# Strassen matrix product on one core: when s4's quarter sums are made, and a fourth sum of s3 that goes through DRAM

## The chip, the cores and the metric

One core of a Trainium2 chip runs the kernel. The metric is the device time of one launch in microseconds; the runs shown are three, with their median. Engines are named as the profile names them: PE is TensorE (matmuls; its weight loads are PEld), DVE is VectorE, ACT is ScalarE, POOL is GpSimd, SP is SyncE, which here only issues DMAs.

## The reference

```python
m, k, n = 4096, 4096, 4096          # a, b: float32, alpha = 0.01
def reference(a, b, alpha):
    x = np.matmul(a, b)
    return np.where(x > 0, x, alpha * x)
```

## The kernel before

The product is computed in float16 with float32 sums. The output is cut into four groups of 1024 rows (g = 0 to 3) and four strips of 1024 columns (j = 0 to 3). One group and one strip together are a region; its product has the full inner size of 4096. A region is computed by the Winograd form of Strassen's method: A's part is cut into a11, a12, a21, a22 and B's part into B11, B12, B21, B22, and seven products of half the size take the place of eight. The sums of A are s1 = a21 + a22, s2 = s1 - a11, s3 = a11 - a21 and s4 = a12 - s2; those of B are made in place. The list PRODUCTS gives the order: a11, a12, s2, s3, s1, a22, s4. A whole product is 64 matmuls of 128x512 (some 13.8 us). Three of the seven can be split once more by the same method, "in quarters": seven small products of 16 matmuls of 128x256 (12.2 us). That is done for product 3 (s3) in `fourth_in_quarters`, product 5 (a22) in `sixth_in_quarters` and product 6 (s4) in `seventh_in_quarters`. Each needs four quarter sums of its A operand (sx[1] to sx[4]) and three of its B operand (t(2), t(4), t(1)). The products are numbered from 0, as in the code.

The loop over `regions` is unrolled. Within a group the order of strips is 2, 0, 3, 1 (in the last group 2, 0, 1, 3). The text names a region (g, j). The first regions of a group are (1,2), (2,2) and (3,2), the second ones (1,0), (2,0) and (3,0). In a first region product 3 is whole; in the second and third, and in the fourth of groups 1 and 2, it is in quarters.

Nothing is reordered by a scheduler: the pools are under a manual schedule, each engine runs its instructions in the order in which the code issues them, and a wait is put where a tile's earlier writers or readers demand it. So an instruction that waits holds up everything behind it on its engine or DMA queue. DMAs are issued from three queues: SP (stores of the output, what is kept in DRAM and brought back), ACT (the loads of s4's kept sums) and POOL (A and B from the inputs, converted to float16 on the way). All of them share 16 DMA engines.

What the change touches:

- `sums_of_a(g, name, room)` makes the four quarter sums of a22 or s4 on DVE (L700, 128x2048 each) and stores each on SP into `kept_q` in DRAM (L701). `room(n)` gives the tile for sum n. The later products load the sums from DRAM: a22's by `load_sums` on SP, s4's by `following` within `sixth_in_quarters` on ACT (both L743).
- `new_a16()` takes a tile of 512 KB from a pool of three that also serves the loads of A and the squares of the measures. `x_pool` holds three tiles of 2 MB: s1, s2 and s4; after product 2, s2's place becomes `t`, four quarter tiles t[:, 0] to t[:, 3], for quarter sums of B and one of A.
- `keep_x21` stores a quarter of s4 or a22 to DRAM in groups 1 and 2 (L716), since its place is used for s3's sums.
- `sums_of_s3` makes s3's quarter sums (L734): 1 and 3 at the end of a first region, 2 and 4 in the second. The fourth is stored on SP (`kept_s3`, L736); the third and fourth regions load it from there (L1071, L1108), the second region uses it from where it was made.
- `b_sum` (L588) makes the sums of B: behind product 0 the two of B12 and then those of B11 that become t2, the operand of product 2 (two halves, `ks`; product 2 takes them one after the other); behind product 1 B21; behind product 2 the operand of product 4. `t3_of_b` (L680) and `sums_of_b` (L686, L688, L690) make the quarter sums of B.
- `measure` objects square tiles of B on ACT (L230) and add them up on DVE (L239 to L263), for a check of the values' sizes. `early` are those around product 0 (one in (1,0), two in (2,0), none in (3,0)), `middle` the one behind it (in (3,0): B22).
- `leave(u1_pairs, 0, 0)` applies the leaky ReLU (L312) to what product 1 finished (L967 adds the banks) and stores it in four DMAs on SP (L978).
- `load_s2` (L770) brings s2 back from DRAM in two halves, the second behind the first sum of B. `fetch_b` issues the sixteen loads of the next region's B from POOL (L532), four for each of B12, B11, B21, B22 in this order, as soon as the products free their places.

Of the kernel before, what the change touches and what calls it, by code (L numbers as in the profile page):

```python
# [47 lines left out]
def kernel(  # L48
# [402 lines left out]
    for i in range(1, len(steps)):  # L451
        t, h, u, first, last = steps[i]
# [19 lines left out]
        t, h, u, first, last = steps[i]  # L472
# [117 lines left out]
    def measure(i, which, x, y):  # L590

        if which:
            tiles = [have_b[i, 2 * x + k, y] for k in ((1, 0) if regions[i][0] else (0, 1))]
        else:
            tiles = [at[regions[i][0], x, 2 * y + k] for k in range(2)]
        parts = halves(tiles[0]) + halves(tiles[1])
        if tiles[0] is first_a:
            return MeasureFirst(which, parts, None)
        return Measure(which, parts, not which)
# [71 lines left out]
    def quarters_of_b(i, half, nt):  # L671
        return {(k, n): have_b[i, 2 * half + k, nt][:, :, n * HALF:(n + 1) * HALF]
                for k in range(2) for n in range(2)}

    def quarters_of_a(g, name):
        return {(h, k): operand(g, name, k)[:, :, h * HALF:(h + 1) * HALF, :] for h in range(2) for k in range(2)}

    def t3_of_b(y):

        nc.vector.tensor_tensor(y[0, 1], y[1, 1], y[0, 1], SUB)  # L680

    def sums_of_b(y, to, some=(2, 4, 1)):
        tt = nc.vector.tensor_tensor
        f = lambda n: b_quarter(to[n])
        if 2 in some:
            tt(f(2), y[0, 1], y[0, 0], ADD)  # L686
        if 4 in some:
            tt(f(4), y[1, 0], f(2), SUB)  # L688
        if 1 in some:
            tt(f(1), y[1, 1], f(2), SUB)  # L690

    def sums_of_a(g, name, room):

        x = {key: q.rearrange("p c m e -> p c (m e)") for key, q in quarters_of_a(g, name).items()}
        made = {}

        def make(n, x0, x1, op):
            made[n] = room(n)
            f = lambda t: made[t].rearrange("p (c m) -> p c m", m=2 * HALF) if isinstance(t, int) else x[t]
            nc.vector.tensor_tensor(f(n), f(x0), f(x1), op)  # L700
            nc.sync.dma_start(kept_q[name][n - 1], made[n])  # L701

        make(1, (1, 0), (1, 1), ADD)
        make(2, 1, (0, 0), SUB)
        make(3, (0, 0), (1, 0), SUB)
        make(4, (0, 1), 2, SUB)

    def x21(g, name):
        return operand(g, name, 0)[:, :, HALF:, :]

    def by_chunk(t):
        return t.rearrange("p c m e -> p c (m e)") if len(t.shape) == 4 else t.rearrange("p (c m) -> p c m", m=2 * HALF)

    def keep_x21(g, name):
        if g < G - 1:
            nc.sync.dma_start(by_chunk(kept_x21[name]), by_chunk(x21(g, name)))  # L716
# [7 lines left out]
    def sums_of_s3(g, some, room=None):  # L724

        x = {key: by_chunk(q) for key, q in quarters_of_a(g, "s3").items()}
        rooms = s3_rooms(g)
        sx = {n: by_chunk(room) for n, room in rooms.items()}
        for n in some:
            if n == 4:  # L730
                sx[4] = by_chunk(room)
            x0, x1, op = {1: (x[1, 0], x[1, 1], ADD), 2: (sx[1], x[0, 0], SUB),
                          3: (x[0, 0], x[1, 0], SUB), 4: (x[0, 1], sx[2], SUB)}[n]
            nc.vector.tensor_tensor(sx[n], x0, x1, op)  # L734
            if n == 4:
                nc.sync.dma_start(kept_s3, room)  # L736

    def s3_rooms(g):
        return {1: x21(g, "a22"), 2: x21(g, "s4"), 3: x21(g, "s3")}
# [22 lines left out]
    def new_a16(_=None):  # L762
        return a16_pool.tile([P, QUARTER], DT, name="q16", tag="a16")
# [18 lines left out]
    for i, (g, j) in enumerate(regions):  # L782
# [210 lines left out]
        def fetch_a(h, half, n):  # L993
            if n == 0:
                coming["rows", h, half] = small_pool.tile([P, 16], FP32, name="rows", tag=f"rows{half}")
            coming[h, half][n][0]()
# [21 lines left out]
        first_of_group = i == 0 or regions[i - 1][0] != g  # L1018
        in_quarters = g > 0 and not turning
        in_fourth = in_quarters and not first_of_group  # L1020
        second_of_group = in_fourth and regions[i - 2][0] != g
        early = [measure(i, *block) for block in EARLY.get((g, j), [])]
# [8 lines left out]
        for n, m in enumerate(early):  # L1031
            if n:
                m.begin()
            m.end()
        have_t2 = g > 1 and j == CACHED
        if have_t2:
            for k in ks:
                t = have_b[i, k, 0] = b_pool.tile([P, KC, NT], DT, name="b", tag="b11")
# [28 lines left out]
        if in_fourth:  # L1067
            tq = {n: new_a16() for n in (2, 4)}
            sx4 = new_a16()
            if not second_of_group:  # L1070
                nc.sync.dma_start(sx4, kept_s3)  # L1071
            t3_of_b(quarters_of_b(i, 0, 1))
            sums_of_b(quarters_of_b(i, 0, 1), tq, (2,))
            if second_of_group:
                sums_of_s3(g, (4,), sx4)
            sums_of_b(quarters_of_b(i, 0, 1), tq, (4,))
        if (g, j) == (0, LAST):
# [7 lines left out]
        if turning and g:  # L1085
            t3_of_b(quarters_of_b(i, 0, 1))
            for n in range(3):
                fetch_a(0, 1, n)
        if first_of_group and g:
            keep_x21(g, "s4")  # L1090
            sums_of_a(g, "s4", new_a16)
        if not g:
            bring_a(0, 1)

# [4 lines left out]
        if g:  # L1099
            t = x_pool.tile([P, 4, QUARTER], DT, name="q", tag="x")  # L1100
# [10 lines left out]
        if late_ones:  # L1111
            late_ones[0].end()
        if in_quarters and first_of_group:
            sq = {4: t[:, 3]}
            sums_of_a(g, "a22", lambda n: sq.setdefault(n, sq[4] if n == 4 else new_a16()))
            keep_x21(g, "a22")
# [106 lines left out]
    with tc.If(even == 0):  # L1223
        for m in range(M // RM):
            a_blocks = []
            for u in range(KU):
                t = a_pool.tile([P, KC // 2, RM, 2], BF16, name="a", tag=f"a{u // 2 + 1}{m % 2 + 1}")
# [6 lines left out]
            for n in range(N // NT):  # L1234
                banks = [new_bank(n % 2 * 4 + mt) for mt in range(MT)]
                cols = slice(n * NT, (n + 1) * NT)
                for u in range(KU):
                    t = b_pool.tile([P, KC, NT], BF16, name="b", tag=f"b{u // 2 + 1}{n % 2 + 1}")
# [8 lines left out]
                for mt in range(MT):  # L1247
                    t = c_pool.tile([P, 2, NT], FP32, name="c", tag=f"c{side}")[:, 0]
# [44 lines left out]
```

## Time and profile before

| | us |
|---|---|
| median of 3 runs (lowest, highest) | 1535.87 (1535.59, 1536.5) |
| the profiled execution | 1535.54 |
| its span, first to last instruction | 1533.3 |
| PE busy | 1522.8 (99%) |
| DVE busy | 1157.9 (76%) |
| ACT, POOL busy | 427.0, 282.6 |
| one 128x512 matmul in a row of them | 0.216 (13.81 us for 64) |
| one DVE sum of 128x4096 (L588), of 128x2048 (L700, L734) | 2.29, 1.22 |
| HBM read, written | 361.76 MB, 106.43 MB |

Times in the views are microseconds from the span's first instruction. A line of a timeline gives start, duration, engine, source line, operation, tiles and a count; in square brackets stands how long the engine was idle before it and what ended the wait. A line of waits gives who waited, for whom, the total, how often and the longest. A line of the chain of waits gives start, duration and who, backwards from what ended last. A line of a stretch gives its bounds and length, the busy time of PE, PEld, DVE, ACT and POOL, the granted clock, the busy share of the DMA engines and their GB/s. Buffer numbers are left out of tile names: "s" can be s2 or s4, "kept_qs" are s4's kept sums, "kept_qa" a22's, "kept_s" is either s2's or s3's place in DRAM.

### The profile page before, as it was taken

To read this page: it belongs to the slowest core of one execution; us is meant where nothing else is said; L and a number is where in the kernel's file an instruction comes from. 1 tells how busy PE (TensorE), PEld (TensorE's weight loads), DVE (VectorE), ACT (ScalarE), POOL (GpSimd) and SP (SyncE) were. 2 spreads that over 40 slices of the span, in tenths; PEclk is the share of its full clock that TensorE was granted. 3 is DMA by queue.
4 is the path that set the end of the run, shared out by engine and by line. 5 is a ranking of instruction groups with operands and counts; after the bars stand their busy time and mean duration, and the time that the engine had idled before them with its cause. 6 is when DMAs were issued, how large, how long until landed. Compare 5 with 4: busy or idle time off the path is not lost. (4 is left out here: it accounts for less than half of the span.)

```text
span 1533.3 us, 21827 instructions
## 1 busy us (share of the span) xinstructions
PE 1522.8 (99%) x8667; PEld 846.6 (55%) x8667; DVE 1157.9 (76%) x1207; ACT 427.0 (28%) x730; POOL 282.6 (18%) x458
## 2 busy tenths in 40 slices
PE   9999999999999999999999999999999999999998
PEld 4444444444446567574544747557544475746656
DVE  4368867766699686768769798686977968787497
ACT  2201344647310213103651130312464113041210
POOL 5641110143202011022220202010331110101100
PEclk9999999999999999999999999999999999999999
DMA  9999895998869979599798979969899895948934
GB/s 246 188 212 205 238 282 168 181 193 175 239 277 282 246 178 276 139 290 256 168 282 273 283 186 210 260 157 322 167 240 295 225 282 138 286 170 191 275 123 140
DMA packets 205442, 342.87 MB, mean 224 GB/s; under 512 B 18833, under 2 KB 148113, under 8 KB 195346
## 3 DMA queue, kind: packets, MB, share of 16 engines
q0 software_dynamic: 136704, 129.00, 52.9%
q1 hardware_dynamic: 62002, 186.81, 33.2%
q10 hardware_dynamic: 6624, 25.56, 4.5%
q8 instruction: 70, 1.15, 0.3%
q14 instruction: 42, 0.34, 0.1%
HBM read 361.76 MB, written 106.43 MB: 305 GB/s over the span
## 5 line engine op out<-in xcount | busy, mean ns | idle before, releaser
L801 PE MATMUL ps<-b,a 128*128 128x512 f16 x2624 | 570.7, 379 | 0.1
L801 PE MATMUL ps<-b,s 128*128 128x512 f16 x2240 | 489.2, 379 | 0.0
L801 PEld LDWEIGHTS <-a 128*128 128x128 f16 x2624 | 256.8, 98 | 307.9 <-issue 0.4
L801 PEld LDWEIGHTS <-s 128*128 128x128 f16 x2240 | 219.1, 98 | 262.7 <-issue 0.4
L588 DVE TENSOR_TENSOR b<-b 128x4096 f16<-128x4096 f16 x104 | 235.0, 2288 | 67.9 <-DMA b<-in_b_dram 59.2
L532 POOL DMA_DIRECT2D b<-in_b_dram x160 | 118.8, 747 | 862.4 <-PE ps L751 324.2
L814 ACT COPY c<-ps 128x512 f32<-128x512 f32 x164 | 84.8, 598 | 443.7 <-PE ps L801 374.6
L141 DVE STREAM_TRANSPOSE a<-a 128x512 uint32<-128x512 uint32 (+2 forms) x120 | 126.8, 1106 | 99.6 <-DMA a<-in_a_dram 99.6
L132 POOL DMA_DIRECT2D a<-in_a_dram x252 | 137.8, 553 | 264.8 <-ACT junk L607 94.7
L751 PEld LDWEIGHTS <-q 128*128 128x128 f16 x1424 | 139.3, 98 | 17.4 <-issue 0.8
L607 ACT ACTIVATE junk<-a 128x512 bf16<-128x512 f16 x192 | 121.5, 633 | 97.1 <-DMA a<-in_a_dram 91.8
L312 DVE SCALAR_TENSOR_TENSOR c<-c 128x1024 f32<-128x1024 f32 (+2 forms) x123 | 141.7, 1194 | 3.3 <-ACT c L814 3.1
L230 ACT ACTIVATE sq<-b 128x2048 bf16<-128x2048 f16 x64 | 119.3, 1911 | 61.4 <-DVE sq L239 41.7
L751 PEld LDWEIGHTS <-a 128*128 128x128 f16 x1200 | 117.4, 98 | 17.7
L967 DVE TENSOR_TENSOR c<-ps,c 128x512 f32<-128x512 f32 x140 | 87.5, 682 | 42.5 <-PE ps L801 29.9
L282 PE MATMUL ps<-b,a 128*128 128x512 f16 x512 | 112.2, 379 | 0.6 <-ACT a L379 0.2
L751 PE MATMUL ps<-b,q 128*128 128x256 f16 x784 | 92.0, 273 | 0.9 <-DVE c L856 0.6
L751 PE MATMUL ps<-b,a 128*128 128x256 f16 x752 | 88.3, 273 | 0.0
L282 PEld LDWEIGHTS <-a 128*128 128x128 f16 x512 | 49.7, 98 | 60.9 <-issue 1.6
L903 ACT COPY c<-ps 128x512 f32<-128x512 f32 x9 | 5.3, 588 | 269.9 <-PE ps L751 181.7
L751 PEld LDWEIGHTS <-s 128*128 128x128 f16 x624 | 61.1, 98 | 7.1
L856 DVE TENSOR_TENSOR c<-ps,c 128x512 f32<-128x512 f32 x80 | 52.3, 685 | 13.5 <-PE ps L751 13.5
(104 smaller groups left out, 903.3 us busy)
## 6 DMA issues: line engine op xcount, KB each, us to landing
b<-in_b_dram POOLq DMA_DIRECT2D x168, 512.0 KB, 13.3
out_dram<-c SPq DMA_DIRECT2D x240, 256.0 KB, 6.1
a<-in_a_dram POOLq DMA_DIRECT2D x244, 128.0 KB, 5.8
b<-kept SPq DMA_DIRECT2D x20, 1024.0 KB, 9.1
q<-kept_qs ACTq DMA_DIRECT2D x40, 512.0 KB, 7.7
s<-kept_s SPq DMA_DIRECT2D x18, 1024.0 KB, 7.4
q<-kept_qa SPq DMA_DIRECT2D x28, 512.0 KB, 7.6
b<-kept_last SPq DMA_DIRECT2D x12, 1024.0 KB, 11.1
```

The source lines that it names most:

```text
L132: nc.gpsimd.dma_start(a16[32 * q:32 * q + 32], src.rearrange("(g i) w -> i g w", i=32))
L141: nc.vector.transpose(part.rearrange("p c m e -> p c (m e)").bitcast(U32) .rearrange("p c (g i) -> p g c i", i=32), src[:, :, i * n:(i + 1 ...
L230: nc.scalar.activation(to, self.parts[n], SQUARE)
L282: nc.tensor.matmul(ps, a_cols(at[0, h, u], c, mt, (h, u) == (0, 0)), bt[0, u, nt][:, c, :], start=first, stop=last,)
L312: nc.vector.scalar_tensor_tensor(t, t, alpha, t, op0=MULT, op1=MAX if alpha <= 1 else MIN)
L532: nc.gpsimd.dma_start(t[:, c:c + 4, :], b_rows(j, u, c, 4, nt, g > 0))
L588: nc.vector.tensor_tensor(f(to), f(x0), f(x1), op)
L607: nc.scalar.activation(junk, piece[:, q, :], SQUARE, accum_out=to[:, 4 * n + q:4 * n + q + 1])
L751: nc.tensor.matmul(to[m], xq[:, c // 2, rows, c % 2], yq[:, c, :], start=first and c == 0 and m < banks, stop=c == KC - 1, skip_group_chec ...
L801: nc.tensor.matmul(banks[mt], a_cols(t, c, mt, t is first_a), B(half, nt, k)[:, c, :], start=first and (k, c) == todo[0], stop=(k, c) == t ...
L814: nc.scalar.copy(kept[mt], banks[mt])
L967: nc.vector.tensor_add(to, bank, to)
```

## The change

In the first region of groups 1 to 3, `keep_x21(g, "s4")` and `sums_of_a(g, "s4", ...)` move from ahead of product 2 to behind it, past the two L588 sums for product 4, to just ahead of a22's sums. The sums no longer take tiles from the pool of three; they lie in `t`, that is in s2's place. Sums 1, 2, 3, 4 go to t[:, 3], t[:, 0], t[:, 2], t[:, 1], which a22's fourth sum and the quarter sums of B21 write next.

In second regions with fewer than two early measures, (1,0) and (3,0), s3's fourth sum is made and stored right behind product 0 and its early measure, into a tile of the pool; where it was made before, behind product 1, the tile `sx4` is now loaded from DRAM, on SP.

```diff
@@ behind product(0, y, True), sums_of_s3(g, (2,)) and the early measures
+        s3_whole = second_of_group and len(early) < 2
+        if s3_whole:
+            sums_of_s3(g, (4,), new_a16())
         have_t2 = g > 1 and j == CACHED
@@ behind product(1, z, True), add(u1, z) and leave(u1_pairs, 0, 0)
         if in_fourth:
             tq = {n: new_a16() for n in (2, 4)}
             sx4 = new_a16()
-            if not second_of_group:
+            if s3_whole or not second_of_group:
                 nc.sync.dma_start(sx4, kept_s3)
             t3_of_b(quarters_of_b(i, 0, 1))
             sums_of_b(quarters_of_b(i, 0, 1), tq, (2,))
-            if second_of_group:
+            if second_of_group and not s3_whole:
                 sums_of_s3(g, (4,), sx4)
             sums_of_b(quarters_of_b(i, 0, 1), tq, (4,))
@@ ahead of product(2, y, False)
-        if first_of_group and g:
-            keep_x21(g, "s4")
-            sums_of_a(g, "s4", new_a16)
@@ behind product 2 and the two sums for product 4
         if in_quarters and first_of_group:
+            keep_x21(g, "s4")
+
+            sums_of_a(g, "s4", lambda n: t[:, {1: 3, 2: 0, 3: 2, 4: 1}[n]])
             sq = {4: t[:, 3]}
             sums_of_a(g, "a22", lambda n: sq.setdefault(n, sq[4] if n == 4 else new_a16()))
             keep_x21(g, "a22")
```

The load of `sx4`, L1071 before, is L1074 in the changed kernel.

## The prediction

> **What bounds the kernel now.** I read the busy shares, then TensorE's waits, then the chain of waits, then the two kinds of region that the change touches, on VectorE's timeline, TensorE's and the DMA engines'.
>
> ```profile
> PE 1522.8 (99%) x8667; PEld 846.6 (55%) x8667; DVE 1157.9 (76%) x1207; ACT 427.0 (28%) x730; POOL 282.6 (18%) x458
> ```
> ```profile
> PE ps L751 <- DVE c L856: 0.6, 1, 0.6
> PE ps L751 <- DVE q L734: 0.3, 1, 0.3
> ```
> TensorE is the bound, at a granted clock of 0.999. Behind the start-up it waits twice, 0.9 us in all: at 489.4 in region (1,2) and at 1295.8 in (3,0). Nothing that a change to other engines removes can be worth much more; what it can cost has no such limit. So the question is what lies close behind TensorE. The chain of waits, on the way to the second wait:
>
> ```profile
> 1251.65 24.03 DMA b<-in_b_dram
> ...
> 1280.41 1.23 DVE sq L239
> ...
> 1287.51 2.48 DVE c L967 x4
> ...
> 1292.26 1.15 DVE b L680
> ...
> 1294.65 1.15 DVE q L734
> 1295.80 0.05 issue
> 1295.85 8.91 PE ps L751 x80
> ```
> The last load of B lands at 1275.68, and from there VectorE works without a pause to L734, s3's fourth sum: 20.2 us from landing to TensorE. VectorE's timeline in (1,0) and TensorE's next to it:
>
> ```profile
> 527.91 2.29 DVE L588 TENSOR_TENSOR b<-b 128x4096 f16<-128x4096 f16 x1 [8.33 <-DMA b<-in_b_dram]
> ...
> 530.29 2.29 DVE L588 TENSOR_TENSOR b<-b 128x4096 f16<-128x4096 f16 x1
> ```
> ```profile
> 532.98 13.98 PE L801 MATMUL ps<-b,s 128*128 128x512 f16 x64
> ```
> VectorE sat 8.33 us waiting for B; t2 (the sum ending 532.58) was ready 0.4 us before product 2 began. Here too a B load sets the time. Why are those loads late? Three stretches of (3,2), with DMA share and GB/s as last columns:
>
> ```profile
> 1199.00:1202.00 3.00, 3.00 (x15) 1.37 (x14) 2.96 (x3) 0.99 (x3) 0.00 (x0) 1.00 0.00 0
> 1202.00:1208.00 6.00, 6.00 (x29) 2.74 (x28) 5.60 (x5) 0.00 (x0) 1.50 (x2) 1.00 0.90 350
> 1208.00:1269.00 61.00, 61.00 (x395) 38.48 (x393) 39.60 (x42) 8.37 (x13) 10.38 (x14) 1.00 1.15 263
> ```
> Ahead of 1202 the DMA engines are idle; 1202 to 1208 they carry s4's sums to DRAM; from 1208 to the last B load they are never idle (over 1 means packets overlap). The sixteen B loads of the next region are issued from 1205.75 on and queue for 25 us. So a store that moves from before 1208 to behind it makes those loads land later by its own time.
>
> **Part A: s4's four sums and stores, three regions.** VectorE's timeline in (3,2):
>
> ```profile
> 1195.85 4.50 DVE L588 TENSOR_TENSOR b<-b 128x4096 f16<-128x4096 f16 x2
> 1200.25 1.23 DVE L700 TENSOR_TENSOR q<-s 128x2048 f16<-128x2048 f16 x1
> ...
> 1205.42 4.49 DVE L588 TENSOR_TENSOR b<-b 128x4096 f16<-128x4096 f16 x2
> ```
> Four sums of 1.22 us now follow the two L588 sums for product 4. These can start at once (product 2 ended at 1198.4), so they run 1200.25 to 1204.7 and s4's sums 1204.7 to 1209.3; VectorE's total is unchanged. The waits of L700 for a free a16 buffer go: 3.5 us in (1,2), 0.4 in each of the others. That is worth the 0.6 us at 489.4, where VectorE was late, and nothing elsewhere. a22's fourth sum and the three of B21 now wait for s4's stores to leave their room: each comes 7 to 8 us after its store, and such stores land after 2.7 us alone, 5.8 (median) in traffic; VectorE has 2.5 and 2.8 us to spare ahead of L967 in (2,2) and (3,2). I take 0. keep_x21's store stays where it was on SP: it waits for sum_a alone, and SP's order does not change. The loads of s4's sums (ScalarE's queue, from 1229.7) come long after. Behind the four stores SP holds only a22's, due from 1210 as before.
>
> The stores move 4.4 us later. In (3,2) they were issued 1201.51 to 1205.85 and had nearly all gone before B's data started near 1208; now the first is issued at about 1206 and 3.5 of 4 fall into the busy stretch. In (2,2) (issues from 829.27, B's first load issued 833.14) 3 of 4 move. In (1,2) (458.48; 459.60) two stores were in it already: 2 move.
>
> **What a store costs B's loads.** Alone, SP's queue moved 1.83 MB in the 4.6 busy us of 1202 to 1207, so 0.52 MB takes 1.3 us. From the other side, the fourteenth B load landed 68.2 us after the first was issued in (1,2) and 64.3 us in (2,2), with 7.92 against 6.84 MB on SP's queue in between: 3.9 us for two stores, 1.9 each. The third stretch, (3,2), had 0.55 MB less than (2,2) and was shorter by 0.5 us: 0.5 for a store. I take 1.4, nearest to the store timed by itself; 0.5 and 1.9 are the ends.
>
> **Part B: s3's fourth sum in (1,0) and (3,0).** One sum of 1.2 us moves into the 8.3 and 11.9 us for which VectorE waited there (free), and leaves the row at 1294.65 (1.14 us less behind the landing). (2,0) has two measures ahead and keeps its order. The store moves from 545.9 and 1295.8 into the busy stretch: 1.4 us more on B's loads. It stands ahead of load_s2 on SP, but leaves 8 us and more before that. New is a load (L1074), on SP behind the four stores of leave(u1): the same sequence as in the third regions, where
>
> ```profile
> 1002.22 1.96 SPq L978 DMA_DIRECT2D out_dram<-c  x4
> 1004.27 0.41 SPq L1071 DMA_DIRECT2D q<-kept_s  x1
> ```
> ```profile
> DMA to landing us min/median/max: 3.8/3.8/3.9
> ```
> it lands 3.8 us after issue, all four times. In (1,0) it would be issued at 543.3 and land at 547.1, 3 us ahead of sx[4]'s use (third quarter product, 546.79 + 3.5). In (3,0) the stores are issued from 1291.15, so the load goes at 1293.2 and lands at 1297.0; TensorE wants it at 1295.4. L743's four loads behind it wait for TensorE anyway.
>
> The Trainium skill, "DMA: Bandwidth & Descriptors", section "Anatomy of one DMA", gives 2.0 us plus bytes over 436 GB/s, an estimated 3.2 us for this load; the rows here say 3.8. By the page the sum below would be 0.6 us less.
>
> **Sum.** (1,0): 2 stores and s3's, 3 x 1.4 = 4.2 us later; t2 ends at 536.8, product 2 starts 3.9 us later than at 532.98. The 0.6 us won at 489.4 is lost in this wait. (2,0): 3 x 1.4 = 4.2; its B load lands at 897.5 (issued 872.06, 25.4 us) and L588 begins at 900.78 behind the measure, so 3.3 us are hidden; t2 (903.16 + 2.29) ends 0.15 us ahead of product 2. That leaves 0.75, and the measure, which squares B21 ahead of L588, is late with its last tile by some 0.5: +1.2. (3,0): 4.5 stores, 6.3 us, less 0.4 for engine time idle near 1217, so 5.9; the landing moves to 1281.6, the stores' issue begins 15.5 us behind it and the load lands 5.9 us behind that (2.05 to its issue, 3.8 to landing), at 1303.0 where TensorE started at 1295.85: +7.1 (product 2's wait of 2 us is inside this). Nothing later waits, so all of it reaches the end: 3.9 + 1.2 + 7.1 = +12.2 on the profiled execution's 1535.54, 1547.7; that execution lies 0.3 below the median 1535.87, so 1548.
>
> **Rivals.** (a) *The whole cost, as summed*: 1548. (b) *Only B's transfers cost; the backlog takes up s4's stores*, as the cheap pair (0.5 us) suggests: (1,0) 1.4 - 0.4 = +1.0, (3,0) 1.4 + 1.2 = +2.6, with 0.3 for the rest, 1540. Against it: no idle DMA time in the stretch. (c) *Not slower*: the stores fit between B's packets, B lands as before, and L1074's load is hidden. Then only the waits go, -0.9: 1535. If the load alone is late, 1297.0 for 1295.85, it is +1.2 - 0.6: 1536.5. It decides if B's loads land within 1 us of before. For it: TensorE waited nowhere for B's data alone, and 0.5 us a store is one of the pairs. Against it: the rows of 1208 to 1269. The Trainium skill's same page, "Rules for kernel authors", says to issue a DMA early and wait for it late, so that its fixed cost overlaps; by that rule the round trip is hidden and this rival comes true. In (3,0) the rows leave 2.2 us for a load that takes 3.8. (d) *Worse*: the stores share the engines with B's first loads and land after 9 to 12 us (the longest L701 row is 11.9), so VectorE waits for t's room, loses its 2.5 us and stalls the sixth product in (2,2) and (3,2) by about 2 us each: 1552.
>
> **Chances.** (a) 0.60, (b) 0.17, (c) 0.13, (d) 0.10. 0.2%, 3.1 us, is about what a measurement here can tell. Every removable wait adds up to less than that, so faster gets 0.02 (out of (c)); (c)'s rest and the low edge of (b) make the same 0.14; slower 0.84. Range: with 0.5 us a store the sum is 1.1 + 0 + 3.4 = +4.5 (1540), with 1.9 it is 5.3 + 2.4 + 9.3 = +17 (1553); it goes 1.5 further down for a store that costs nothing in (1,0); (c) is left out below. (a)'s own range is 1542 to 1553.
>
> **What would show it.** Right: in (1,0) and (3,0) TensorE waits some 4 and 2 us for L588's t2 at product 2, and in (3,0) some 5 us more for the load of kept_s3; B's last load in (3,2) takes about 30 us instead of 24.0; the wait at 489.4 gone or harmless. Wrong: B's landings where they were (then (c)); waits of L686 or L700 on kept_qs in the first regions that reach TensorE (then (d)).

## The result, and the profile after

| | us |
|---|---|
| before, median of 6 runs (lowest, highest) | 1535.73 (1533.47, 1536.5) |
| after, median of 6 runs (lowest, highest) | 1549.06 (1547.47, 1554.65) |
| ratio after/before, 95% interval | 1.0096 (1.0079 to 1.0113) |
| the profiled execution of after, its span | 1548.70, 1546.6 |
| predicted | 1548.0 (1538.5 to 1553) |

The change makes the kernel 13.3 us slower. The busy times of the page, which answer to the first line shown of before:

```profile
PE 1528.0 (99%) x8667; PEld 847.9 (55%) x8667; DVE 1158.7 (75%) x1207; ACT 426.4 (28%) x730; POOL 282.0 (18%) x458
```

No engine does more work: VectorE is busy 0.8 us longer for the same 1207 instructions. TensorE is busy 5.2 us longer for the same 8667 matmuls, which is odd; most of it is explained below. The rest is waiting. TensorE's waits, in all, times, longest:

```profile
PE ps L801 <- DMA b<-in_b_dram: 4.7, 4, 3.5
PE ps L751 <- DMA q<-kept_s: 4.0, 1, 4.0
PE ps L801 <- DVE b L588: 1.2, 2, 0.8
...
PE ps L751 <- DVE c L967: 0.6, 1, 0.6
```

Before, none of these lines was there. Where they are, from TensorE's timeline of after:

```profile
505.26 1.89 PE L801 MATMUL ps<-b,a 128*128 128x512 f16 x8 [0.64 <-DMA b<-in_b_dram]
510.64 27.75 PE L801 MATMUL ps<-b,a 128*128 128x512 f16 x120 [3.49 <-DMA b<-in_b_dram]
885.29 26.06 PE L801 MATMUL ps<-b,a 128*128 128x512 f16 x120 [0.32 <-DMA b<-in_b_dram]
911.83 13.97 PE L801 MATMUL ps<-b,s 128*128 128x512 f16 x64 [0.48 <-DVE b L588]
...
1286.26 13.97 PE L801 MATMUL ps<-b,s 128*128 128x512 f16 x64 [0.77 <-DVE b L588]
1300.81 3.65 PE L751 MATMUL ps<-b,a 128*128 128x256 f16 x32 [0.57 <-DVE c L967]
1308.45 2.70 PE L751 MATMUL ps<-b,q 128*128 128x256 f16 x16 [3.99 <-DMA q<-kept_s]
```

Two kinds of wait are as forecast, and both are shorter: the sums of B at product 2 of (3,0) (0.77 us, about 2 in the prediction; 0.48 in (2,0)), and the load of kept_s3 (3.99 us, about 5 in the prediction). The largest wait for B is not at product 2 of (1,0) but at its product 0, which reads B11 itself.

Two rows are longer than their work. 16 matmuls of 128x256 take 1.91 us elsewhere, and 2.70 behind the wait at 1308.45; 120 of 128x512 take 26.06 us at 885.29, and 27.75 at 510.64. Stretches of after around both (columns as in the table of the front: busy PE, PEld, DVE, ACT, POOL, then granted clock, DMA share, GB/s):

```profile
507.30:510.71 3.41, 0.07 (x1) 0.07 (x1) 3.41 (x5) 0.33 (x2) 0.00 (x0) 1.00 1.11 318
510.71:514.12 3.41, 3.41 (x9) 1.24 (x9) 2.27 (x2) 3.41 (x2) 0.74 (x1) 0.50 1.21 232
...
1306.02:1309.43 3.41, 0.98 (x9) 0.89 (x10) 3.41 (x3) 0.58 (x1) 0.00 (x0) 1.00 0.34 137
1309.43:1312.84 3.41, 3.41 (x18) 2.44 (x17) 3.41 (x3) 0.00 (x0) 1.39 (x2) 0.50 0.19 52
```

After each of the two waits the granted clock is 0.50 for 3.41 us. In that time TensorE does half of the work, so each wait costs 1.7 us more than its length. That is 3.4 of the 5.2 us of busy time that TensorE gained. Some 1.0 more is the end of the last matmul ahead of a wait, of which there are six more than before: 8 matmuls that start 0.216 us apart take 1.89 us, 0.16 more than eight times that, and this end counts as busy time only where no matmul follows at once. The remaining 0.8 was not looked into.

The chain of waits in (3,0), the part that answers to the one shown of before:

```profile
1259.67 26.78 DMA b<-in_b_dram
...
1291.17 1.23 DVE sq L239
...
1304.29 4.11 DMA q<-kept_s
1308.40 0.05 issue
1308.45 10.57 PE ps L751 x80
```

B's last load takes 26.78 us instead of 24.03, and L1074's load, 4.11 us, stands directly ahead of TensorE. From B's landing (1286.45) to TensorE's start it is 22.0 us; before it was 20.2.

Where the 13.3 us arise can be read from the start of the same product in both traces, after minus before: product 2 of (1,0) +5.24 (532.98 to 538.22), of (2,0) +6.23, of (3,0) +8.17, product 4 of (3,0) +14.14 (1304.72 to 1318.86). 0.8 of it comes back by the end, which looks like an accident of the trace of before: behind VectorE's last instruction it runs on for 5.3 us, that of after for 4.2, and all but one of the others for 4.0 to 4.5.

### The profile page after: what moved, and what is told of

Its sections match the earlier page's. It is cut to its first block, busy times and chain, and to the rows that moved or that the text cites. A ratio compares the mean times of both kernels' runs of the same rounds, so it can differ in the third digit from the quotient of the medians.

```text
span 1546.6 us, 21829 instructions
## 1 busy us (share of the span) xinstructions
PE 1528.0 (99%) x8667; PEld 847.9 (55%) x8667; DVE 1158.7 (75%) x1207; ACT 426.4 (28%) x730; POOL 282.0 (18%) x458
## 4 chain that ended last, share of the span: by engine, by line
PE 85%; DMA 12%; DVE 1%; ACT 1%; issue 1%; POOL 0%; SPq 0%; ACTq 0%; POOLq 0%; DVEq 0%
PE ps L801 60%; PE ps L751 18%; DMA b<-in_b_dram 8%; PE ps L282 7%; DMA a<-in_a_dram 2%; ACT junk L607 1%; DMA a_in<-in_a_dram 0%; DVE b L588 0%; DMA q<-kept_s 0%; POOL a L132 0%; DVE c L312 0%; DVE c L967 0%; PE turned L372 0%; ACT c L814 0%; ACT sq L230 0%
## 5 line engine op out<-in xcount | busy, mean ns | idle before, releaser
L588 DVE TENSOR_TENSOR b<-b 128x4096 f16<-128x4096 f16 x104 | 234.8, 2287 | 71.1 <-DMA b<-in_b_dram 66.5
L814 ACT COPY c<-ps 128x512 f32<-128x512 f32 x164 | 84.6, 596 | 442.9 <-PE ps L801 375.3
```

The costliest lines, as they stand in the source:

```text
L588: nc.vector.tensor_tensor(f(to), f(x0), f(x1), op)
L814: nc.scalar.copy(kept[mt], banks[mt])
```

## The experiments

The theory, T: the stores of s4's sums stand among the loads of B instead of ahead of them, so B lands later, and in (3,0) a round trip through DRAM stands behind that. The rivals: V, VectorE's new order makes things late; L, the round trip is the larger part; H, the load is hidden. C is a theory of its own, on what the half clock costs. For each run the table has the same reading as above, starts minus those of before, and the time from product 2 to product 4 of (3,0). The ratio is against runs of the kernel before that were taken along with it; their medians are the range in the first line.

| kernel | (1,0) p2 | (2,0) p2 | (3,0) p2 | (3,0) p4 | p2 to p4 in (3,0) | median us | ratio (95%) |
|---|---|---|---|---|---|---|---|
| before | 0 | 0 | 0 | 0 | 26.63 | 1534.4 to 1535.9 | 1 |
| after | 5.24 | 6.23 | 8.17 | 14.14 | 32.60 | 1549.1 | 1.0096 (1.0079 to 1.0113) |
| stores alone | 5.32 | 11.22 | 11.23 | 12.81 | 28.21 | 1548.8 | 1.0090 (1.0071 to 1.0109) |
| sum of s3 alone | 0.98 | 0.95 | 1.85 | 2.49 | 27.27 | 1537.9 | 1.0021 (1.0007 to 1.0035) |
| early load | 6.21 | 12.68 | 14.08 | 15.66 | 28.21 | 1547.0 | 1.0072 (1.0055 to 1.0090) |
| short stores | 5.94 | 6.31 | 6.31 | 6.90 | 27.22 | 1541.4 | 1.0050 (1.0034 to 1.0067) |
| matmuls in the wait | 5.29 | 7.88 | 7.88 | 12.11 | 30.86 | 1546.2 | 1.0075 (1.0055 to 1.0096) |
| before, more stores | 11.96 | 16.30 | 16.74 | 19.01 | 28.90 | 1553.7 | 1.0130 (1.0113 to 1.0147) |
| order of B11 | 2.11 | 7.98 | 10.26 | 17.44 | 33.81 | 1548.6 | 1.0085 (1.0069 to 1.0102) |
| room alone | 3.88 | 3.87 | 3.87 | 3.28 | 26.04 | 1536.5 | 1.0012 (1.0000 to 1.0024) |
| after once more | 3.57 | 4.61 | 4.95 | 12.18 | 33.86 | 1552.4 | 1.0125 (1.0108 to 1.0142) |
| early load, order of B11 | 2.15 | 6.37 | 9.93 | 11.49 | 28.19 | 1543.9 | 1.0062 (1.0045 to 1.0079) |
| place undone | 5.28 | 5.26 | 5.26 | 4.67 | 26.04 | 1536.2 | 1.0011 (0.9997 to 1.0025) |

The trace of a kernel is one execution, the median several. After and its variants scatter by up to 7 us from run to run, and the table shows where: mostly in (2,0).

### The stores alone

```diff
-        s3_whole = second_of_group and len(early) < 2
+        s3_whole = False
```

> The changed kernel with only its first part: s4's sums and stores behind the sums of B, but s3's fourth sum made where it was before, with no load. Theory T (the stores that moved behind B's loads are what costs): (1,0) keeps the whole of its 5.1 us, with both waits of product 0 for B11, since s3's store came only after them; (2,0) +1.0, (3,2) +0.6; in (3,0) the last B load lands some 3.8 us later than before (5.0 in the changed kernel, less one store) and VectorE's 20.2 us from landing to L734 follow: +3.7. Sum +10.4 on 1535.7: 1546. Rival L (the round trip of s3's sum is half of the cost): TensorE's first stall of (3,0) is gone and the time is 1541 to 1542.

Measured: 1548.8 us, as slow as the whole change. TensorE's timeline:

```profile
512.41 26.06 PE L801 MATMUL ps<-b,a 128*128 128x512 f16 x120 [3.17 <-DMA b<-in_b_dram]
883.94 1.89 PE L801 MATMUL ps<-b,a 128*128 128x512 f16 x8 [0.61 <-DMA b<-in_b_dram]
889.24 27.75 PE L801 MATMUL ps<-b,a 128*128 128x512 f16 x120 [3.41 <-DMA b<-in_b_dram]
1308.66 1.92 PE L751 MATMUL ps<-b,q 128*128 128x256 f16 x16 [1.88 <-DVE q L734]
```

(1,0) is as in the changed kernel. (3,0) costs 1.6 us and not 3.7: L734 is late by 1.9 us, with no load. What had not been expected is (2,0), where product 0 now waits 4.0 us and the clock is halved behind it, +5.9 in all; there the code is that of the changed kernel, whose trace had 0.3 us. So L falls for the whole, and something in (2,0) differs between executions.

### The sum of s3 alone

```diff
 ahead of product(2, y, False)
+        if first_of_group and g:
+            keep_x21(g, "s4")
+            sums_of_a(g, "s4", new_a16)
 behind product 2's sums
-            keep_x21(g, "s4")
-            sums_of_a(g, "s4", lambda n: t[:, {1: 3, 2: 0, 3: 2, 4: 1}[n]])
```

> The changed kernel with only its second part: s4's sums and stores back where they were before; s3's fourth sum behind product 0 in (1,0) and (3,0), and the load of it. Theory T: in (1,0) product 2 waits 0.8 us (one store of 1.2 us, 0.4 us to spare), product 0 no more than the 0.24 us of before; in (3,0) the landing is 1.2 us later and the load lands 21.4 instead of 20.2 us behind it: +2.4, and up to 1.7 more if the clock is halved behind that wait. Sum +3.2 to +4.9: 1539 to 1540.5. Rival L: 1542 to 1543. Rival H (the load is hidden here, since its lateness came from the stores of s4): within 1 us of before, 1536.

Measured: 1537.9, ratio 1.0021 (1.0007 to 1.0035). Against its own runs of the kernel before (1534.7) that is +3.2 us, the lower end of T's +3.2 to +4.9; the time itself lies below the 1539 that T named, which was counted from 1535.7.

```profile
507.00 26.06 PE L801 MATMUL ps<-b,a 128*128 128x512 f16 x120 [0.59 <-DMA b<-in_b_dram]
533.96 13.97 PE L801 MATMUL ps<-b,s 128*128 128x512 f16 x64 [0.90 <-DVE b L588]
1298.47 1.92 PE L751 MATMUL ps<-b,q 128*128 128x256 f16 x16 [1.06 <-DMA q<-kept_s]
```

The 0.90 at product 2 of (1,0) goes with the fourteenth load, which lands 69.2 instead of 68.2 us behind the first issue: one store. In (3,0) the load costs 0.6 us (27.27 against 26.63) and not 2.4. H falls, though by little. The two parts do not add up in (3,0): the stores alone cost 1.6 there, the sum of s3 alone 0.6, both together 6.0 and 7.2 (two traces). The rows of the first of these show the terms. Behind its first issue, B's last load lands 1.6 us later than before in the stores alone, 0.6 earlier in the sum alone, and 4.0 later in the whole change, of which TensorE had already lost 1.4 by product 2. From that landing to TensorE the load from DRAM adds 1.4 in the sum alone and 1.8 in the whole, and only the whole has a half clock behind it, 1.7. That gives 1.6, 0.8 and 6.1.

### The load issued early

```diff
+        if s3_whole:
+            sx4 = new_a16()
+            nc.sync.dma_start(sx4, kept_s3)
         product(1, z, True)
...
-            sx4 = new_a16()
-            if s3_whole or not second_of_group:
+            if not s3_whole:
+                sx4 = new_a16()
+            if not second_of_group:
```

> The changed kernel with the load of sx4 issued on SP behind product 1's matmuls but ahead of the four stores of what it finished (it needs neither). Theory T: the wait of 3.99 us in (3,0) for kept_s3 goes, and the half clock behind it, 1.7 us: 1549.1 - 5.7 = 1543.4. Rival L (all of the transfers compete, so the load lands late wherever it stands, or VectorE's sums for the quarter products are then as late as the load was): a wait of 2 us or more stays at that place, for kept_s or for VectorE, and the time is 1546 or more.

Measured: 1547.0. T's expectation for the place was met; its time, 1543.4, was not, and 1547.0 is the time that rival L named, without the wait that L named for it.

```profile
885.57 1.89 PE L801 MATMUL ps<-b,a 128*128 128x512 f16 x8 [1.35 <-DMA b<-in_b_dram]
890.70 27.75 PE L801 MATMUL ps<-b,a 128*128 128x512 f16 x120 [3.24 <-DMA b<-in_b_dram]
...
1312.63 1.91 PE L751 MATMUL ps<-q,a 128*128 128x256 f16 x16 [0.52 <-DVE q L688]
1320.38 13.97 PE L801 MATMUL ps<-b,s 128*128 128x512 f16 x64 [0.59 <-DVE b L588]
```

The wait for kept_s and its half clock are gone; VectorE is now late by 0.5 and 0.6 us, and (3,0) from product 2 to product 4 is 28.21 instead of 32.60: 4.4 us won. But (2,0) again has the wait at product 0 (4.6 us and a half clock, +6.5).

That wait goes with a race in (2,2): how early SP issues the first store of s4's sums against POOL's first load of B. From the traces' DMA issues (the first load's issue is zero):

| kernel | first s4 store issued | eighth B load lands | product 0 of (2,0) waits |
|---|---|---|---|
| room alone | -5.2 | 39.9 | 0 |
| before | -3.9 | 41.7 | 0 |
| after once more | -1.2 | 47.2 | 0.6 |
| matmuls in the wait | -1.0 | 49.1 | 2.6 |
| after | -0.7 | 46.9 | 0.3 |
| stores alone | +0.7 | 50.7 | 4.0 |
| early load | +1.4 | 51.3 | 4.6 |
| short stores | +1.5 | 40.8 | 0 |

With the first store some 4 us and more ahead of the load, the eighth load lands at 40 to 42 us; 0.7 to 1.2 us ahead, at 47 to 49; behind it, at 51. The order at the issue does not fix it alone: the three traces with the store 0.7 to 1.2 us ahead lie 2.2 us apart and not in the order of their issues. The last line, with the stores as late but short, shows that it is their bytes. No run moved the moment of the issue alone, so that the race makes the difference is argued from this table. That the slow ones among the runs of the changed kernel (1551 to 1555) have this wait is argued too, from the three other traces with the same code in (2,2), which wait 2.6, 4.0 and 4.6 us; neither trace of the changed kernel itself had more than 0.6.

### Short stores

```diff
-            nc.sync.dma_start(kept_q[name][n - 1], made[n])
+            cut = QUARTER // 16 if name == "s4" and g > 1 else QUARTER
+            nc.sync.dma_start(kept_q[name][n - 1][:, :cut], made[n][:, :cut])
```

> The changed kernel in which the four stores of s4's sums write only the first sixteenth of each row in groups 2 and 3 (group 1 whole), so that products of those groups use stale sums and the output is not the reference's; instructions, order, waits and places are otherwise the same. Theory T (bytes in the way of B's loads): (1,0) stays as in the changed kernel (product 0 waits 1.89 and 3.49 us, half clock); B's loads in (2,2) and (3,2) land 4 to 5 us earlier, (2,0)'s +1.0 goes, and in (3,0) the 7.5 us shrink to 1 to 2 us: 1549.1 - 6.5 to - 7.5, so 1542. Rival V (it is VectorE's new order, with the sums between L588 and a22's sums, that makes things late): no change, 1549.

Measured: 1541.4, by T 1542, by V 1549. The waits of this run:

```profile
511.73 27.35 PE L802 MATMUL ps<-b,a 128*128 128x512 f16 x120 [3.11 <-DMA b<-in_b_dram]
1302.88 1.92 PE L752 MATMUL ps<-b,q 128*128 128x256 f16 x16 [1.01 <-DMA q<-kept_s]
```

(1,0), where the stores are whole, is as in the changed kernel (+5.9); from there to product 2 of (2,0) only 0.4 us are added instead of 1.0 to 6.5, and (3,0) costs 0.6 instead of 6.0. B's sixteenth load lands 69.4 us behind the first issue in (2,2) and 69.5 in (3,2); with whole stores at about the same places it is 74.6 (early load) and 73.9 (after): 4.4 to 5.2 us for 3.75 stores, 1.2 to 1.4 us each. V falls.

### The kernel before, with four more stores

```diff
             keep_x21(g, "a22")
+            for n in range(4):
+                nc.sync.dma_start(extra[n], whole_s[g, "s1"].rearrange("p k c m e -> p (k c m e)")[:, n * QUARTER:(n + 1) * QUARTER])
```

> The kernel before with four more stores of 512 KB (of s1, to a place in DRAM that nothing reads) on SP behind a22's stores in (1,2), (2,2) and (3,2); VectorE's work and its order are those of the kernel before. Theory T (a store among B's loads costs 1.2 us): B's loads land 4 to 5 us later; in (1,0) product 0 waits 3 to 5 us for B11, in (2,0) +1 to +1.5, in (3,0) +4.8: 1534.7 + 10 to 12, so 1545 to 1547. Rival V (VectorE's order is what costs): 1535, and no wait for B.

Measured: 1553.7, by T 1545 to 1547, by V 1535.

```profile
503.49 2.34 PE L752 MATMUL ps<-q,q 128*128 128x256 f16 x16 [3.02 <-ACT c L904]
516.30 28.80 PE L802 MATMUL ps<-b,a 128*128 128x512 f16 x120 [4.02 <-DMA b<-in_b_dram]
...
896.00 26.06 PE L802 MATMUL ps<-b,a 128*128 128x512 f16 x120 [3.46 <-DMA b<-in_b_dram]
...
1314.86 1.92 PE L752 MATMUL ps<-b,q 128*128 128x256 f16 x16 [2.15 <-DVE q L735]
```

With VectorE's order that of before, the same waits appear at the same places: product 0 of (1,0) and of (2,0), and L734 (here L735) in (3,0). V falls a second time. The extra time has a cause of its own: in (1,2) ScalarE waited for a store of the output to leave its tile, and TensorE for ScalarE, 3.02 us. That the four stores had made those behind them on SP late is the likely reason; it was not tried.

### The room alone

```diff
+        if in_quarters and first_of_group:
+            keep_x21(g, "s4")
+            sums_of_a(g, "s4", lambda n: t[:, {1: 3, 2: 0, 3: 2, 4: 1}[n]])
         for k in ks:
             b_sum(B(0, 0, k), B(1, 1, k), B(0, 0, k), SUB)
```

with the same two lines gone from behind that loop, and `s3_whole = False`.

> The changed kernel's room alone: s4's sums in s2's place as in the changed kernel, but made ahead of the two sums of B for product 4, so that their stores go out as early as in the kernel before; s3's fourth sum as in the kernel before, no load. Theory T (place among the loads costs, room does not): B's loads land within 1 us of before, the 0.6 us at 489.4 go: 1534 to 1535. Rival D (a22's fourth sum and the sums of B21 wait for the stores to leave their room): waits of L686 to L700 for kept_qs that stall the sixth product by 1 to 2 us in (2,2) and (3,2): 1537 to 1539.

Measured: 1536.5, ratio 1.0012 (1.0000 to 1.0024), ten runs from 1533.4 to 1539.7. TensorE's one wait for data between start-up and end:

```profile
509.61 27.42 PE L801 MATMUL ps<-b,a 128*128 128x512 f16 x120 [3.33 <-DMA b<-in_b_dram]
```

D falls: no wait for kept_qs reaches TensorE, and VectorE has none on L686 to L700. T holds for B's last load, which lands within 0.2 us of before in (1,2) and (2,2) and 2 us earlier in (3,2); for the time it does not, as 1536.5 lies between the two forecasts. The wait at 489.4 of before is gone, 0.8 us. But in (1,2) the first store is issued 0.3 us ahead of B's first load and not 1.1, and the eighth load lands 49.9 us behind the first issue instead of 47.4: the wait for B11. That the one makes the other is likely and was not tried. The runs lie in two groups of five, 1533.4 to 1535.4 and 1537.6 to 1539.7; the trace is of the second, and the first has none.

### The order of B11's halves, and with the early load

```diff
-        fetch_b(i + 1, [(0, 0)], ks)
+        fetch_b(i + 1, [(0, 0)], (1, 0) if in_quarters else ks)
```

> The changed kernel with the loads of B11 for (1,0), (2,0) and (3,0) issued in the order in which those regions' product 0 uses the two halves (second half first; in the kernels so far the first comes first). Theory T: in (1,0) product 0's waits of 1.89 and 3.49 us and the half clock behind them go; product 2 waits some 1.8 us for t2 instead (the fourteenth load lands 2.2 us later than before, 0.4 us to spare): (1,0) costs 1 to 2 us, not 5.1, and the waits at product 0 in (2,0), where there are any, go too: 1544 to 1546. Rival O (the order does not matter, since the wait moves whole to product 2): 1549.

Measured: 1548.6, as O said.

```profile
535.09 15.44 PE L801 MATMUL ps<-b,s 128*128 128x512 f16 x64 [2.61 <-DVE b L588]
...
913.58 15.63 PE L801 MATMUL ps<-b,s 128*128 128x512 f16 x64 [2.64 <-DVE b L588]
...
1310.69 3.60 PE L751 MATMUL ps<-b,q 128*128 128x256 f16 x16 [4.15 <-DMA q<-kept_s]
```

The waits at product 0 are gone, and t2 is late instead, with a half clock behind it (15.44 and 15.63 us for 64 matmuls that take 13.97). (1,0) costs 2.1 instead of 5.2; what it won is lost here in the other regions. With both remedies:

> The changed kernel with both remedies: the load of sx4 ahead of the four stores, and B11's halves in the order of use. Theory T: the early load takes 4 to 4.5 us off (3,0) (as between the traces of the changed kernel and of the run with the early load); the order of B11 alone gave -1.7 us in (1,0), since t2 was late at product 2 instead. What stays is B's late landing: 1549.1 - 5 to - 6, so 1543 to 1544. Rival R (the gains trade places again: what is won at one wait is lost in the next): 1546 or more.

Measured: 1543.9, ratio 1.0062 (1.0045 to 1.0079), as T said; the four runs lie within 3.6 us.

```profile
911.97 15.47 PE L801 MATMUL ps<-b,s 128*128 128x512 f16 x64 [2.50 <-DVE b L588]
1288.02 13.97 PE L801 MATMUL ps<-b,s 128*128 128x512 f16 x64 [1.33 <-DVE b L588]
```

What stays, 9.4 us, are mostly the sums of B, late because B lands late, and two half clocks behind them.

### Matmuls in the wait

```diff
+            if second_of_group and g == G - 1:
+                for _ in range(16):
+                    nc.tensor.matmul(third, w[:, :P], w, start=True, stop=True)
```

> The changed kernel with sixteen extra 128x512 matmuls (3.5 us, into a bank that the next product starts anew) put in front of the quarter product that waits for sx4 in (3,0), so that TensorE works while the load is under way. Theory C (the clock record of 0.5 behind this wait is caused by TensorE's idle time in the 3.41 us before it, and costs 1.7 us): no record of 0.5 near 1309, the sixteen matmuls of the quarter product take 1.91 us and not 2.70, and product 4 starts 1.7 us sooner against product 2's start than in the changed kernel (31.1 instead of 32.77 us). Rival: the halving has another cause, or the record does not change the matmuls' times; then 32.8 us stay. The whole time moves by less than the runs of one kernel differ here.

Measured: 1546.2 (two runs).

```profile
1308.09 1.92 PE L751 MATMUL ps<-b,q 128*128 128x256 f16 x16 [0.77 <-DMA q<-kept_s]
```

The product's row is 1.92 us instead of 2.70, there is no half clock near it, and product 2 to product 4 is 30.86 instead of 32.60: C holds, 1.7 us. (The 32.77 of the expectation took the start in the chain of waits, 1319.03.)

### The changed kernel again

> The changed kernel itself once more, with more runs, to see what differs between its executions. Expected: 1547 to 1554, median 1549. In (1,0) product 0 waits 1 to 2 and 3 to 3.5 us for B11 as in every run with the stores behind. In (2,0) it depends on which comes first in (2,2): with the first store of s4 issued before the first load of B (0.7 us in the trace of the changed kernel) the eighth load lands some 47 us behind the first issue and product 0 waits 0.3 us; with the store 0.6 to 1.4 us behind the load (as in the run with the stores alone and in the one with the early load) 51 us, and 3 to 4.5 us of waiting. The clock is halved for the next 3.41 us whenever TensorE was idle for more than some 2.1 us of a grid stretch of 3.41 us, and not where a wait is cut in two by the grid. Rival: all of this is fixed by the program, and the trace shows the waits of the first one.

Measured: median 1552.4, four runs from 1546.8 to 1554.3; over both sets ten runs, 1546.8 to 1554.7. The trace is of the fastest.

```profile
510.65 26.06 PE L801 MATMUL ps<-b,a 128*128 128x512 f16 x120 [3.19 <-DMA b<-in_b_dram]
883.92 26.06 PE L801 MATMUL ps<-b,a 128*128 128x512 f16 x120 [0.61 <-DMA b<-in_b_dram]
```

The wait in (1,0) is there, and this time no half clock follows it (26.06 us, not 27.75); the half clock behind the load of kept_s3 in (3,0) lasts 6.8 us here. In (2,2) the first store was 1.2 us ahead of B's first load, and (2,0) waits 0.6 us. The rival falls: the program does not fix these waits.

### The place undone

The early load and the place of "the room alone" in one kernel: of the change everything is kept but the place of s4's sums and, of the load, its place.

> The changed kernel with everything kept but the place of s4's sums: they lie in s2's room, but are made ahead of the two sums of B for product 4, so that their stores go out early; s3's fourth sum stays in product 0 and comes back from DRAM, its load ahead of the four stores. Theory T: the place of the stores is 11 to 12 of the 13 to 14 us; here B's loads in (2,2) and (3,2) land within 2 us of before, and what is left is the wait for B11 in (1,0), which came with the room alone too (3.3 us and a half clock, in some executions): 1535 to 1539. Rival L (the round trip through DRAM costs some 4 us by itself, and the early load does not hide it): 1540 or more.

Measured: 1536.2, ratio 1.0011 (0.9997 to 1.0025), ten runs from 1534.1 to 1540.2. TensorE waits in (1,0) alone:

```profile
505.56 1.89 PE L801 MATMUL ps<-b,a 128*128 128x512 f16 x8 [0.88 <-DMA b<-in_b_dram]
510.68 27.75 PE L801 MATMUL ps<-b,a 128*128 128x512 f16 x120 [3.23 <-DMA b<-in_b_dram]
```

(3,0) takes 26.04 us from product 2 to product 4, 0.6 less than before. So the place of the stores, with what it does to the load behind them, makes nearly all of the cost. No version here beats the kernel before; TensorE's waits there leave about 1 us to win.

## Why the prediction was right, and where it was not

The time (1548.0 for 1549.1) and the likeliest case (a) came true: B's loads land later because stores stand among them, and the round trip stands behind that. That the time came within 1.1 us is in part luck. One wait was looked for at the wrong product, terms that were off made up for each other in (3,0), and what (2,0) costs differs from execution to execution: four more runs of the same kernel had a median of 1552.4. By its steps:

- **(1,0), +3.9: measured +5.1 and +3.7 (two traces; starts of product 2, less the entry's offset), but not where it said.** The step that failed is "t2 ends at 536.8, product 2 starts 3.9 us later". The price was sought at VectorE, the reader of B11 that was seen waiting. TensorE reads B11 too, in product 0: eight matmuls and then the rest wait for the seventh and eighth load, which carry the half that it takes first. Having waited there (4.1 us), it was no longer waiting at product 2. The load that the step counted on, the fourteenth, lands only 2.2 us later and not 4.2, so that the total for (1,0) came near by luck. The profile of before showed it in one row, product 0 and 1 of (1,0) beside those of (2,0):

```profile
505.11 28.03 PE L801 MATMUL ps<-b,a 128*128 128x512 f16 x128
...
877.85 27.79 PE L801 MATMUL ps<-b,a 128*128 128x512 f16 x128
```

  128 matmuls take 27.79 us; those at 505.11 took 0.24 more. That was a wait for the eighth load, landing at 507.04, too short to be listed: nothing to spare.
- **(2,0), +1.2: measured +1.0 in both traces of the changed kernel, 2.6, 5.9 and 6.5 in three others with the same code there.** The sum had one outcome of several. Its argument, how many of the four stores come before B's first load, pointed at the right place; that a difference of 2 us at the issue goes with some 4 us of waiting was not seen.
- **(3,0), +7.1: measured 7.3 and 7.6, of it 6.0 and 7.2 from product 2 to product 4.** Its terms were off and made up for each other in the first trace: the landing moved by 4.0 us and not 5.9 (73.9 instead of 69.9 us behind the first issue; B's last load took 26.8 us and not about 30), TensorE started 22.0 us behind it (the prediction had the load land 21.4 behind it), and the half clock, 1.7, was not in the sum.
- **1.4 us for a store: right as a price (1.2 to 1.4 by the short stores), too high as used.** Against before, the sixteenth load lands 3.5 us later in (2,2) for 3 stores and 4.0 in (3,2) for 4.5: 0.9 to 1.2 each. Part of that is a gain that the sum left out: in (2,2) the first data of B flow 1.8 us behind the first issue instead of 2.6, since fewer stores are ahead of them. In (3,2), where the price was lowest, they flow at 2.7 instead of 2.2, so there the low price stays open.
- **Part A's room at 0: right.** In the trace of after VectorE waited for kept_qs 0.6 us in (2,2) and 2.8 in (3,2) (L686 to L690), and none of it reached TensorE; its own room alone made no such wait. So (d) did not come, though its premise did: the last of the four stores landed 8.9 and 11.0 us after its issue. The 2.8 us are all that the prediction gave VectorE to spare in (3,2).
- **The 0.6 at 489.4 "lost in the next wait": right.** The wait is gone, and (1,0) begins 0.8 us earlier only to wait for B.
- **(b) and (c).** A cost of the transfers alone does not hold: with both parts (3,0) loses some 4.4 us more than with the load issued early. (c)'s own sign, B's loads within 1 us of before, did not come: the sixteenth lands 2.3, 3.5 and 4.0 us later in (1,2), (2,2) and (3,2). (c)'s rule from the Trainium skill ("DMA: Bandwidth & Descriptors", section "Rules for kernel authors": issue a DMA early, wait late) is borne out by the early load; in the changed kernel the load is issued late, behind what product 1 leaves. The 3.2 us that the prediction worked out from the Trainium skill ("DMA: Bandwidth & Descriptors", section "Anatomy of one DMA") are an estimate for a DMA that POOL issues; this load is issued by SP, behind four stores, and took 4.1 us in (3,0).
- **+0.6 in (3,2) of the first trace**, in no term of the sum: two matmuls of product 1 start 0.49 us behind the one before instead of 0.22, each released by a copy of ScalarE (L814). The sum of s3 alone has three of these, the second trace of the changed kernel none. Why ScalarE was late was not looked into.
- **The range.** Its low end takes 1.5 us off (1,0) for stores that cost nothing, where the sum at 0.5 us a store had only 1.1 there: 1539 and not 1538.5.

## What to carry to other kernels

Before a store is moved, look which loads will queue beside it, and list every reader of what they bring, TensorE's own first: a row that is 1% longer than its equals is a wait with nothing to spare. DMA time that lies idle ahead of a burst of loads is worth as much as the stores that can go there. A round trip through DRAM can be hidden by issuing the load ahead of the stores that it does not need; if it is issued last, it adds its whole length to whatever made the issue late.

## What the runs showed of the hardware

**Half a clock after a wait, and it depends on a grid.** In the thirteen traces 17 waits of TensorE were followed by a granted clock of 0.50, which begins on a grid of 3.413 us: the two in the trace of after are 798.72 us apart, 234 times 3.4133. What decides is TensorE's idle time within one stretch of that grid. Summed over the matmuls' rows, stretches with 2.09, 2.15, 2.19 us and more of idle time were followed by a half clock; those with 1.87, 1.92, 1.99 and 2.06 were not. So a wait of 3.17 us that the grid cut in two cost no clock (stores alone: 1.53 and 1.99 idle), and one of 2.61 us did (order of B11). The nearest pair lies in one trace, that of before with more stores:

```profile
501.41:504.82 3.41, 1.33 (x13) 1.19 (x13) 0.67 (x1) 0.59 (x1) 0.74 (x1) 1.00 1.12 313
504.82:508.23 3.41, 3.41 (x19) 2.43 (x17) 0.00 (x0) 0.59 (x1) 0.00 (x0) 0.50 1.12 303
893.94:897.35 3.41, 1.35 (x7) 0.64 (x7) 3.41 (x4) 2.55 (x2) 0.74 (x1) 1.00 1.14 241
897.35:900.76 3.41, 3.41 (x18) 1.52 (x17) 2.66 (x3) 1.91 (x1) 0.00 (x0) 1.00 1.17 262
```

1.33 us busy: half clock next; 1.35 busy: full clock next. The half clock lasted one stretch, or two where TensorE was idle 0.81 us or more in the first of them (0.81, 1.17, 1.19, 1.24; with 0.77 and less it ended). Ends of matmuls are modelled, so the bounds are rough. The Trainium skill, "TensorE: Matmul & The Clock Gate", section "What's actually happening", has the free-running window of 3413 ns and the half rate, and the traces agree; it puts the half rate behind a whole idle window, and here 2.1 us of 3.41 were enough.

**The same program runs in more than one way.** In traces with the same code in (2,2), SP's first store is issued from 1.2 us ahead of POOL's first load to 1.4 us behind it, and the eighth load lands at 47 to 51 us. B's first load in the trace of after, issued at 838.38, and the second store of s4, at 838.93, are in flight together and land at 846.85 and 844.00. From 841 to 843 us the DMA engines moved 115 packets of SP's queue (0.45 MB) and, between them, 147 of POOL's (0.15 MB): the stores' packets are four times as long, and the loads got a quarter of the bytes. The Trainium skill, "DMA: Bandwidth & Descriptors", section "Queues, rings and completion order", says that each DMA engine takes its queues in turn, packet by packet. The trace agrees: about as many packets of either queue in the same 2 us.
